# One vector per kind for the compressed branch's position terms, and tokens laid out by ScalarE straight from PSUM

## The chip, the core and the metric

The kernel runs on one core of one Trainium2 chip. Its time is the device time of one launch in microseconds (us). The profile shows one execution by engine: TensorE (PE, with its weight loads as PEld), VectorE (DVE), ScalarE (ACT), GpSimd (POOL) and SyncE (SP), which here only starts DMAs. A range like "745.00:775.00" is in us from the span's start.

## The reference, cut to what matters

The reference is one decoder layer for 1024 tokens of width 1024: a token mixer with three branches (stick-breaking attention, native sparse attention, a gated linear recurrence), then a feed-forward part that picks rows out of tables of 16384 experts (PEER), then a norm. The change touches one place: in sparse attention, keys and values for the compressed branch are made from overlapping blocks of 32 tokens, 16 apart. A learned position term is added to each block before it is multiplied with a weight:

```python
def compress(x, w):
    pieces = x.reshape(B, G, n_piece, CMP_STRIDE, dh)
    blocks = jnp.concatenate([pieces[:, :, j:j + n_cmp] for j in range(per)], axis=3) + cmp_pe
    return blocks.reshape(B, G, n_cmp, CMP_LEN * dh) @ w

kc = compress(k_cmp, w_cmp_k)
vc = compress(v_cmp, w_cmp_v)
```

Here B is 1, G is 2 (key groups), the head width dh is 64, CMP_STRIDE is 16 and CMP_LEN 32, so that there are 63 blocks, each a row of 2048 numbers times a weight of 2048 by 64. `cmp_pe` has 32 rows of 64 and is the same for every block and both groups.

## The kernel before, in words

**Two stages.** First a mixing stage: the tokens go through in four parts of 256 (`PARTS`), and for each part four rounds `r` of three kinds of items (`hg` the recurrence, `ns` the sparse attention, `sb` the stick-breaking attention) are worked off as a list of small items, while projections, merges, output products, top-k routing and, for parts 1 and 2 of 0 to 3 (`DENSE`), the spreading of the gates (`hot`, `gb`, `stage`) are emitted between them. Then a dense stage: for parts 1 and 2 all 128 blocks of experts are multiplied through (`gemm1`, whose result is the tile `g`, then `gemm2` into `acc`), while parts 0 and 3 have their expert rows gathered by GpSimd (lines 1149 and 1159) and used on VectorE (lines 1151 and 1161).

**What sets the order.** Python code emits the instructions in a planned order: pieces have a step by which they must be out (`before`), and a running account of modelled work for PE and DVE (`account`, `due`) decides how many optional pieces go into each step. The tile framework then schedules what was emitted by a timeline simulation at build time (`schedule_with_timeline_sim=True`, line 1567), so that the order on every engine depends on the modelled duration of everything emitted. At run time each engine works its queue in that fixed order. The VectorE work on gathered rows is placed among the mixing stage's VectorE work by `paced` (line 1119).

**Projections.** `proj` (line 268) loads a weight block in a high and a low half, and adds 24 matmuls of 128 by 256 into a PSUM tile of the pool `ps_mm`, which has two buffers. Such a buffer is free when its reader, mostly one ScalarE copy, is done; the next projection but one needs it.

**The piece that the change rewrites.** `nsa_kv_pieces` (line 470) makes a part's keys and values. `pieces(which)` (line 498, `which` 0 for keys and 1 for values) copies the projection into the tile `xc` (line 486, ScalarE) and then lays it out for the product in `xp` on VectorE (`add_pe`, line 510): 16 slots `j`, each of two tokens in the two halves of the partitions, for both groups and all blocks. Slots 0 to 7 hold a block's first 16 tokens and slots 8 to 15 its last 16, so each token is written twice, with another position term each time. That is eight VectorE instructions per kind and part, and four small ones more from part 1 on, for the 16 tokens kept in `xhist` from the part before (line 521). `compress` (line 523) then multiplies the 16 slots with the weight `cw` into `pk` and copies the result into `kcT` or `vcT` (line 527).

**ScalarE's tables.** The kernel keeps ScalarE on a table that holds exponential and logarithm (`log_exp`, line 95). `sigmoids` (line 889) is the exception: with high priority it applies sigmoids to the recurrence's `raw_hg` and `sg`, to the branch gates `gts` in a part's first round, and to the merge gates `mg`, and then asks for the exp-and-log table again (line 903). Wherever the final ScalarE order puts an exponential or logarithm between two of these sigmoids, a table load (ACT_TABLE_LOAD) stands before it, one for the exponential and another for the logarithm. The logits of stick-breaking attention need both in turn (`e_sb`, exponential at line 423 and logarithm at line 424, then a VectorE scan at line 429, and an exponential at line 433).

Of the kernel before, what the change touches and what calls it, by code (L numbers as in the profile page):

```python
# [10 lines left out]
F32 = mybir.dt.float32  # L11
# [5 lines left out]
AF = mybir.ActivationFunctionType  # L17
ALU = mybir.AluOpType
# [53 lines left out]
def trunk(ctx: ExitStack, tc: tile.TileContext, a: dict, out: bass.AP):  # L72
# [26 lines left out]
    def load(t, src):  # L99
        nc.sync.dma_start(t, src)  # L100
        return t
# [28 lines left out]
    packed = load(cst.tile([128, 273], F32, name="packed"), a["c_packed"])  # L130
    ident, rowv, iota16 = packed[:, 0:128], packed[:, 128:129], packed[:, 129:145]
    forced = packed[:, 145:273].rearrange("p (a b) -> p a b", a=8)
    small = load(cst.tile([128, 40], F32, name="small"), a["small"])
    peT, hnorm, hlb = small[:, 0:32], small[:, 32:36], small[:, 36:40]
    identb = cst.tile([128, 128], BF16, name="identb")
    V.tensor_copy(identb, ident)
    ones = cst.tile([128, 128], F32, name="ones")
# [60 lines left out]
    vcT = per.tile([64, 2, 64], F32, name="vcT")  # L198
    V.memset(kcT, 0.0)
    V.memset(vcT, 0.0)  # L200
    xhist = per.tile([128, 2, 16], F32, name="xhist")
    hgS = [per.tile([128, 128], F32, name=f"hgS{h}") for h in range(4)]
    for h in range(4):
        V.memset(hgS[h], 0.0)
# [265 lines left out]
    def nsa_kv_pieces(pt, st):  # L470
# [25 lines left out]
            st["cw", which] = load(W4(f"cw{which}_{nm}", (128, 16, 64)), a["wcmp"][which])  # L496

        def pieces(which):
            plain(B_NKV + which, f"xc{which}")
            xc = st[f"xc{which}"]  # L500
            xp = st["xp", which] = W2(f"xp{which}_{nm}", (128, 16, 2, np_), tag="xp", bufs=1)

            def add_pe(half, d0, nb, src):
                for g in range(2):
                    gs = slice(g * 64, g * 64 + 64)
                    for par in range(2):
                        o = xp[par * 64:par * 64 + 64, half * 8:half * 8 + 8, g, d0:d0 + nb]
                        i = src[gs].rearrange("p (c j u) -> p u j c", j=8, u=2)[:, par]
                        e = peT[gs, half * 16:half * 16 + 16].rearrange("p (j u) -> p u j", u=2)[:, par]
                        V.tensor_tensor(o, i, e.unsqueeze(2).to_broadcast([64, 8, nb]), op=ALU.add)  # L510


            if pt.first:
                add_pe(0, 0, np_ - 1, xc[:, 0:n - 16])
                add_pe(1, 0, np_ - 1, xc[:, 16:n])
            else:
                add_pe(0, 0, 1, xhist[:, which, :])
                add_pe(0, 1, np_ - 1, xc[:, 0:n - 16])
                add_pe(1, 0, np_, xc)
            if not pt.last:  # L520
                V.tensor_copy(xhist[:, which, :], xc[:, n - 16:n])

        def compress(which, dst):
            pk = ps_mm.tile([64, 2, np_], F32, tag="mm", name=f"pk{which}_{nm}")
            for j in range(16):
                P.matmul(pk[:, :, 0:ncb], st["cw", which][:, j, :], st["xp", which][:, j, :, 0:ncb], start=(j == 0), stop=(j == 15))
            V.tensor_copy(dst[0:64, :, c0:c1], pk[:, :, 0:ncb])

        def turn_values():
            pv = ps_mm.tile([64, 2, 64], F32, tag="mm", name=f"pvc_{nm}")  # L530
# [990 lines left out]
def _layout(inp):  # L1521

    d = {}
    w = np.asarray(inp["w_in"])[0]
    cols = []
    for o, n in ((0, 512), (512, 512), (1024, 512), (1536, 512), (2048, 768), (2816, 24), (2840, 512), (3352, 512), (3864, 512), (4376, 512), (4888, 3072)):
        x = w[:, o:o + n]
        if n == 24:
            x = np.concatenate([x, np.zeros((D, 104), w.dtype)], axis=1)
        cols.append(x)  # L1530
    cols += [np.asarray(inp["w_out"])[0], np.asarray(inp["peer_w_q"])[0]]
    w = np.concatenate(cols, axis=1)
    d["wblk"] = np.ascontiguousarray(w.reshape(8, 128, NBLK, 128).transpose(2, 1, 0, 3))
    br = np.stack([np.asarray(inp[n])[0] for n in ("w_branch_sb", "w_branch_nsa", "w_branch_hgrn")])
    d["wbr"] = np.ascontiguousarray(br.reshape(3, 4, 128, 8, 128).transpose(0, 3, 2, 1, 4).reshape(24, 128, 4, 128))
    cw = np.stack([np.asarray(inp[n])[0].reshape(16, 128, 64).transpose(1, 0, 2) for n in ("nsa_w_cmp_k", "nsa_w_cmp_v")])
    d["wcmp"] = np.ascontiguousarray(cw)
    pe = np.asarray(inp["nsa_cmp_pe"])[0].T
    small = [np.concatenate([pe, pe], axis=0), np.asarray(inp["hgrn_norm"])[0].reshape(4, 128).T, np.asarray(inp["hgrn_lower_bounds"])[0].reshape(4, 128).T]
    d["small"] = np.ascontiguousarray(np.concatenate(small, axis=1))  # L1540
    k = np.asarray(inp["peer_sub_keys"])[0]
    kk = np.zeros((128, 256), k.dtype)
    kk[0:64, 0:128] = k[0].T
    kk[64:128, 128:256] = k[1].T
    d["keysT"] = kk
    d["x"] = np.ascontiguousarray(np.asarray(inp["x"])[0])
    d["norm_mix"] = np.ascontiguousarray(np.asarray(inp["norm_mix"]))
    d["norm_ffn"] = np.ascontiguousarray(np.asarray(inp["norm_ffn"]))
    d["norm_final"] = np.ascontiguousarray(np.asarray(inp["norm_final"])[None])
    d["peer_u"] = np.ascontiguousarray(np.asarray(inp["peer_u"])[0])  # L1550
    d["peer_uT"] = np.ascontiguousarray(d["peer_u"].reshape(128, 128, 8, 128).transpose(0, 3, 2, 1))
    d["peer_v"] = np.ascontiguousarray(np.asarray(inp["peer_v"])[0])
    return d
# [17 lines left out]
```

## Time and profile before

| | |
|---|---|
| median of three runs | 3500.18 us (3494.5 to 3507.36) |
| the profiled execution's own time | 3511.97 us |
| its span, first to last instruction | 3510.2 us |
| PE busy | 3199.7 us, 91% |
| DVE busy | 3000.6 us, 85% |
| ACT busy | 1556.4 us, 44% |
| mean granted TensorE clock | 0.942 |
| first `gemm1` matmul (end of the mixing stage) | 2038.3 us |

Busy times of several engines overlap, so that they do not add up to the span. Matmuls are pipelined and the profile models their ends; an engine's busy share is therefore read stage by stage, beside what it waited for. The chain of waits follows the work back from the last instruction; where it runs through an instruction, that instruction's duration is at that moment what the end hangs on.

### The profile page before, as it was taken

To read this page: it belongs to the slowest core of one execution; us is meant where nothing else is said; L and a number is where in the kernel's file an instruction comes from. 1 tells how busy PE (TensorE), PEld (TensorE's weight loads), DVE (VectorE), ACT (ScalarE), POOL (GpSimd) and SP (SyncE) were. 2 spreads that over 40 slices of the span, in tenths; PEclk is the share of its full clock that TensorE was granted. 3 is DMA by queue.
4 is the path that set the end of the run, shared out by engine and by line. 5 is a ranking of instruction groups with operands and counts; after the bars stand their busy time and mean duration, and the time that the engine had idled before them with its cause. 6 is when DMAs were issued, how large, how long until landed. Compare 5 with 4: busy or idle time off the path is not lost.

```text
span 3510.2 us, 56907 instructions
## 1 busy us (share of the span) xinstructions
PE 3199.7 (91%) x20564; PEld 2175.3 (62%) x20564; DVE 3000.6 (85%) x6666; ACT 1556.4 (44%) x3181; POOL 1361.7 (39%) x1170
## 2 busy tenths in 40 slices
PE   7999889999997799999887889889999999999998
PEld 6887777778886688888565745434444444444443
DVE  6665679888789879889997869999988998998998
ACT  5776455554543554554455233333333333333333
POOL 0000002443332322333231334357765565676672
PEclk9999999999997799999688999989999999999999
DMA  8964856889976588897574998789999999999995
GB/s 305 334 248 147 308 185 226 320 314 310 358 284 231 199 289 291 327 332 259 191 250 154 344 372 312 241 271 387 392 384 329 385 367 362 362 368 375 367 358 219
DMA packets 359283, 1058.00 MB, mean 301 GB/s; under 512 B 35236, under 2 KB 107573, under 8 KB 354391
## 3 DMA queue, kind: packets, MB, share of 16 engines
q0 software_dynamic: 147456, 536.94, 42.5%
q1 hardware_dynamic: 206934, 483.87, 38.7%
q10 hardware_dynamic: 4608, 33.56, 2.5%
q8 instruction: 161, 2.64, 0.3%
q14 instruction: 124, 1.01, 0.1%
HBM read 944.13 MB, written 110.10 MB: 300 GB/s over the span
## 4 chain that ended last, share of the span: by engine, by line
PE 49%; DVE 23%; DMA 11%; issue 8%; ACT 6%; POOL 2%; SPq 0%; DVEq 0%; POOLq 0%; ACTq 0%
PE g L265 13%; PE acc L1441 10%; PE pj_mg L265 4%; DVE u L1151 3%; DVE gacc L1161 3%; PE g L1441 3%; DMA u<-in_peer_u_dram,gidx 3%; PE pj_r_hg L265 2%; DMA v<-in_peer_v_dram,gidx 1%; PE pb L265 1%; DMA gt<-d_G 1%; PE pj_wo L265 1%; POOL v L1159 1%; PE z_sb L417 1%; DMA vraw<-in_peer_v_dram 1%
## 5 line engine op out<-in xcount | busy, mean ns | idle before, releaser
L1159 POOL DMA_INDIRECT v<-in_peer_v_dram,gidx x421 | 556.0, 1321 | 674.0 <-DVE gacc L1161 348.4
L1149 POOL DMA_INDIRECT u<-in_peer_u_dram,gidx x417 | 529.7, 1270 | 596.6 <-DVE u L1151 367.4
L265 PE MATMUL g<-h,us 128*128 128x512 f16 x3072 | 688.2, 381 | 14.8 <-ACT ge L1400 12.1
L1441 PE MATMUL acc<-vs,ac 128*128 128x512 f16 x2304 | 542.2, 383 | 39.9 <-ACT vs L220 23.5
L1441 PEld LDWEIGHTS <-ac 128*128 128x128 f16 x3072 | 303.1, 99 | 426.1 <-issue 66.8
L1161 DVE SCALAR_TENSOR_TENSOR gacc<-v,act,gacc 128x1024 f32<-128x1024 f32 x421 | 538.9, 1280 | 29.4 <-DMA v<-in_peer_v_dram,gidx 25.8
L265 PEld LDWEIGHTS <-us 128*128 128x128 f16 x3072 | 301.6, 98 | 383.0 <-issue 21.1
L1151 DVE SCALAR_TENSOR_TENSOR u<-u,gh 128x1024 f32<-128x1024 f32 x417 | 501.9, 1219 | 33.2 <-DMA u<-in_peer_u_dram,gidx 32.7
L1400 ACT ACTIVATE ge<-g 128x512 f32<-128x512 f32 x128 | 76.1, 596 | 520.7 <-PE g L265 500.1
L265 PE MATMUL pj_mg<-hT,w_mg 128*128 128x256 f16 x2304 | 273.8, 275 | 4.0 <-ACT mg L885 4.0
L265 PEld LDWEIGHTS <-w_mg 128*128 128x128 f16 x2304 | 228.2, 100 | 33.6 <-issue 6.6
L1441 PE MATMUL g<-vs,ac 128*128 128x512 f16 x768 | 190.5, 388 | 11.6 <-ACT ge L1400 11.6
L1149 POOL DMA_INDIRECT rr_u<-in_peer_u_dram,gidx x95 | 134.2, 1413 | 96.7 <-DVE rr_u L1151 49.8
L221 DVE SCALAR_TENSOR_TENSOR vs<-vraw,vs 128x1024 f16<-128x1024 f32 x128 | 154.1, 1219 | 18.6 <-ACT vs L220 18.5
L221 DVE SCALAR_TENSOR_TENSOR us<-uraw,us 128x1024 f16<-128x1024 f32 x128 | 156.1, 1219 | 10.4 <-ACT us L220 10.3
L265 PE MATMUL pb<-o,w_b 128*128 128x256 f16 x1152 | 144.7, 281 | 21.1 <-DVE sg L923 15.1
L1159 POOL DMA_INDIRECT rr_v<-in_peer_v_dram,gidx x90 | 123.0, 1367 | 102.2 <-DVE gacc L1161 81.4
L220 ACT ACTIVATE vs<-vraw 128x1024 f16<-128x1024 f32 x128 | 131.0, 1046 | 55.0 <-DMA vraw<-in_peer_v_dram 55.0
L220 ACT ACTIVATE ac<-ge 128x512 f16<-128x512 f32 x128 | 79.9, 628 | 168.3 <-DVE ge L1434 139.0
L1434 DVE TENSOR_TENSOR ge<-ge,gt 128x256 f32<-128x256 f32 x256 | 98.4, 422 | 58.7 <-ACT ge L1400 44.9
L1223 PE MATMUL gb<-hot 128*128 128x128 f16 x512 | 125.7, 294 | 24.3 <-ACT stage L1226 13.1
L220 ACT ACTIVATE us<-uraw 128x1024 f16<-128x1024 f32 x128 | 134.2, 1048 | 21.4 <-PE g L265 12.8
(1146 smaller groups left out, 6353.8 us busy)
## 6 DMA issues: line engine op xcount, KB each, us to landing
uraw<-in_peer_uT_dram SPq DMA_DIRECT2D x128, 512.0 KB, 7.7
vraw<-in_peer_v_dram SPq DMA_DIRECT2D x128, 512.0 KB, 7.2
w_mg<-dw SPq DMA_DIRECT2D x72, 512.0 KB, 5.8
gt<-d_G SPq DMA_DIRECT2D x32, 1024.0 KB, 17.5
d_G<-stages ACTq DMA_DIRECT2D x20, 1024.0 KB, 5.9
w_r_hg<-dw SPq DMA_DIRECT2D x36, 512.0 KB, 5.4
w_b<-dw SPq DMA_DIRECT2D x72, 256.0 KB, 5.5
wr_mg<-in_wblk_dram SPq DMA_DIRECT2D x24, 512.0 KB, 5.3
```

The lines of the kernel that those rows point to most:

```text
L220: S.activation(hi, src, AF.Copy, scale=scale)
L221: V.scalar_tensor_tensor(lo, in0=src, scalar=scale, in1=hi, op0=ALU.mult, op1=ALU.subtract)
L265: P.matmul(ps, l[:, k, :], r[:, k, :], start=(i == 0), stop=(i == n - 1))
L417: P.matmul(x["z"], qz[:, hh, tl * 128:(tl + 1) * 128], st["k"][:, r0 + c0:r0 + c1], start=True, stop=(c0 > 0))
L1149: G.indirect_dma_start(out=ur, out_offset=None, in_=a["peer_u"], in_offset=bass.IndirectOffsetOnAxis(ap=idx[:, c:c + 1], axis=0))
L1151: V.scalar_tensor_tensor(ur, in0=ur, scalar=1.0, in1=h2, op0=ALU.mult, op1=ALU.mult, accum_out=hpre[:, c:c + 1])
L1159: G.indirect_dma_start(out=vr, out_offset=None, in_=a["peer_v"], in_offset=bass.IndirectOffsetOnAxis(ap=idx[:, c:c + 1], axis=0))
L1161: V.scalar_tensor_tensor(acc, in0=vr, scalar=act[:, c:c + 1], in1=acc, op0=ALU.mult, op1=ALU.add)
L1223: P.matmul(ps[:, n, :], hs[:, 0, :, n], hs[:, 2, :, n], start=True, stop=False)
L1400: S.activation(ge, ps, AF.Gelu, scale=1.0 / (SW * SH2))
L1434: V.tensor_tensor(gv, gv, gt[:, :, i % 8, :], op=ALU.mult)
L1441: P.matmul(ps, ac[:, x, t * 128:(t + 1) * 128], v[:, y, dh * 512:(dh + 1) * 512], start=start and n == 0, stop=stop and n == 2)
```

## The change

The position terms leave the layout. As the product is linear, the 32 position rows times the weight give one vector of 64 numbers per kind, the same for all blocks. It is computed once, in part 0 (`pc`, 16 matmuls with one column each, into `cpos`), and added when the product is taken out of PSUM: `tensor_scalar` in place of a copy, on VectorE as before. Without position terms a token looks the same in both halves of a block, so `xp` has 8 slots in place of 16 and one more column; slot `j` of the weight reads slot `j % 8`, shifted by one column for the second half. The layout is written by four ScalarE copies straight from the projection's PSUM tile, two groups by two token parities, with the scale in the copy, and `xc` is gone. The kept tokens are copied by ScalarE too: out of `xp` into `xhist`, and from there into column 0 of the next part's `xp`.

```diff
         def pieces(which):
-            plain(B_NKV + which, f"xc{which}")
-            xc = st[f"xc{which}"]
-            xp = st["xp", which] = W2(f"xp{which}_{nm}", (128, 16, 2, np_), tag="xp", bufs=1)
-
-            def add_pe(half, d0, nb, src):
-                for g in range(2):
-                    gs = slice(g * 64, g * 64 + 64)
-                    for par in range(2):
-                        o = xp[par * 64:par * 64 + 64, half * 8:half * 8 + 8, g, d0:d0 + nb]
-                        i = src[gs].rearrange("p (c j u) -> p u j c", j=8, u=2)[:, par]
-                        e = peT[gs, half * 16:half * 16 + 16].rearrange("p (j u) -> p u j", u=2)[:, par]
-                        V.tensor_tensor(o, i, e.unsqueeze(2).to_broadcast([64, 8, nb]), op=ALU.add)
...
+            ps = proj(B_NKV + which, hTs[pt.i], f"xc{which}_{nm}", pt)
+            d0 = 0 if pt.first else 1
+            xp = st["xp", which] = W2(f"xp{which}_{nm}", (128, 8, 2, np_ + 1), tag="xp", bufs=1)
+            if not pt.first:
+                S.activation(xp[:, :, :, 0], xhist[:, which], AF.Copy)
+            for g in range(2):
+                for par in range(2):
+                    o = xp[par * 64:par * 64 + 64, :, g, d0:d0 + np_]
+                    S.activation(o, ps[g * 64:g * 64 + 64].rearrange("p (c j u) -> p u j c", j=8, u=2)[:, par], AF.Copy, scale=PS)
             if not pt.last:
-                V.tensor_copy(xhist[:, which, :], xc[:, n - 16:n])
+                S.activation(xhist[:, which], xp[:, :, :, d0 + np_ - 1], AF.Copy)
 
         def compress(which, dst):
             pk = ps_mm.tile([64, 2, np_], F32, tag="mm", name=f"pk{which}_{nm}")
             for j in range(16):
-                P.matmul(pk[:, :, 0:ncb], st["cw", which][:, j, :], st["xp", which][:, j, :, 0:ncb], start=(j == 0), stop=(j == 15))
-            V.tensor_copy(dst[0:64, :, c0:c1], pk[:, :, 0:ncb])
+                P.matmul(pk[:, :, 0:ncb], st["cw", which][:, j, :], st["xp", which][:, j % 8, :, j // 8:j // 8 + ncb], start=(j == 0), stop=(j == 15))
+            if pt.first:
+                pc = ps_mm.tile([64, 1], F32, tag="mm", name=f"pc{which}")
+                for j in range(16):
+                    P.matmul(pc, st["cw", which][:, j, :], pos[:, j:j + 1], start=(j == 0), stop=(j == 15))
+                V.tensor_copy(cpos[:, which:which + 1], pc)
+            V.tensor_scalar(dst[0:64, :, c0:c1], pk[:, :, 0:ncb], cpos[:, which:which + 1], None, op0=ALU.add)
```

Because the order is made at build time, it moves elsewhere too. Three places are shown; lines after the change are those of the changed file, some six lower from line 510 on. In the names, trailing numbers count tiles; `e_sb_3_0_1_512` is a logit tile of part 3, `raw_hg_3` and `mg_3` are that part's recurrence inputs and merge gates.

**VectorE, keys of part 3.** Before:

```order
L221 SCALAR_TENSOR_TENSOR o_2_12357<-tro_ns2g_1_15346,o_2_12357 128x256
L510 TENSOR_TENSOR xp_ns_15480<-xc_ns_15478,small 64x8x15 x4
L510 TENSOR_TENSOR xp_ns_15480<-xc_ns_15478,small 64x8x16 x4
L1161 SCALAR_TENSOR_TENSOR gacc_33005<-v_98_33301,act_32617,gacc_33005 128x1024
L429 SCALAR_TENSOR_TENSOR e_sb_2_0_1_0_15330<-r_sb_2_0_1_0_15333,e_sb_2_0_1_0_15330 128x512
```

and after:

```order
L222 SCALAR_TENSOR_TENSOR o_2_12317<-tro_ns2g_0_15330,o_2_12317 128x256
L222 SCALAR_TENSOR_TENSOR o_2_12317<-tro_ns2g_1_15335,o_2_12317 128x256
L1213 TENSOR_TENSOR hot_15691<-iorep,spread_14070 128x1024
L430 SCALAR_TENSOR_TENSOR e_sb_2_0_1_0_15319<-r_sb_2_0_1_0_15322,e_sb_2_0_1_0_15319 128x512
L1214 TENSOR_TENSOR hot_15691<-hot_15691,spread_14070 128x1024
```

The eight layout instructions are gone, and the gates' spreading (`hot`) moves up into their place.

**ScalarE, sigmoids of part 3's second round.** Before:

```order
L902 ACT_TABLE_LOAD
L902 ACTIVATE raw_hg_3_14885<-raw_hg_3_14885 128x256
L902 ACTIVATE sg_3_17204<-raw_hg_3_14885 128x512
L902 ACTIVATE mg_3_16634<-mg_3_16634 128x1536
L97 ACT_TABLE_LOAD
L421 ACTIVATE e_sb_3_1_0_0_17245<-z_sb_3_1_0_0_17244 128x512
```

and after:

```order
L896 ACT_TABLE_LOAD
L896 ACTIVATE raw_hg_3_14874<-raw_hg_3_14874 128x256
L896 ACTIVATE sg_3_17188<-raw_hg_3_14874 128x512
L424 ACT_TABLE_LOAD
L424 ACTIVATE e_sb_3_0_1_512_17167<-e_sb_3_0_1_512_17167 128x384
L425 ACT_TABLE_LOAD
L425 ACTIVATE e_sb_3_0_1_512_17167<-e_sb_3_0_1_512_17167 128x384
L879 ACTIVATE mg_3_16613<-pj_mg_1_3_16767 128x256
L1220 ACTIVATE stage_16700<-gb_16811 128x128x4
L422 ACTIVATE e_sb_3_1_0_0_17229<-z_sb_3_1_0_0_17228 128x512
L423 ACTIVATE r_sb_3_1_0_0_17232<-z_sb_3_1_0_0_17228 128x512
L424 ACT_TABLE_LOAD
```

The merge gates' sigmoid no longer stands with the two others but 44 rows later, and exponentials and logarithms lie between, each behind a load. ScalarE's queue has 91 table loads before and 108 after; all 17 more are in the mixing stage.

**TensorE, keys of part 0, after:**

```order
L515 MATMUL pk_ns_644<-xp_ns_586,cw_ns_410 64x2x15 x8
L816 MATMUL pa_hg_0_504<-X_hg_0_485 128x64 x2
L515 MATMUL pk_ns_644<-xp_ns_586,cw_ns_410 64x2x15 x8
L816 MATMUL pa_hg_0_513<-X_hg_0_494 128x64 x2
L519 MATMUL pc_661<-small,cw_ns_410 64x1 x16
L816 MATMUL pa_hg_0_598<-X_hg_0_499 128x64 x2
```

The sixteen `pc` matmuls stand behind the sixteen `pk` of the same kind, in part 0 alone. On VectorE's queue 422 uses of gathered rows stand ahead of the dense stage's first product, before as after.

More of the change, by code (lines that the diff above doesn't have):

```diff
@@ L132, in trunk @@
     forced = packed[:, 145:273].rearrange("p (a b) -> p a b", a=8)
-    small = load(cst.tile([128, 40], F32, name="small"), a["small"])
-    peT, hnorm, hlb = small[:, 0:32], small[:, 32:36], small[:, 36:40]
+    small = load(cst.tile([128, 24], F32, name="small"), a["small"])
+    pos, hnorm, hlb = small[:, 0:16], small[:, 16:20], small[:, 20:24]
     identb = cst.tile([128, 128], BF16, name="identb")
@@ L200, in trunk @@
     V.memset(vcT, 0.0)
-    xhist = per.tile([128, 2, 16], F32, name="xhist")
+    xhist = per.tile([128, 2, 8, 2], F32, name="xhist")
+    cpos = per.tile([64, 2], F32, name="cpos")
     hgS = [per.tile([128, 128], F32, name=f"hgS{h}") for h in range(4)]
@@ L498, in pieces @@
         def pieces(which):
-            plain(B_NKV + which, f"xc{which}")
-            xc = st[f"xc{which}"]
-            xp = st["xp", which] = W2(f"xp{which}_{nm}", (128, 16, 2, np_), tag="xp", bufs=1)
-            def add_pe(half, d0, nb, src):
-                for g in range(2):
-                    gs = slice(g * 64, g * 64 + 64)
-                    for par in range(2):
-                        o = xp[par * 64:par * 64 + 64, half * 8:half * 8 + 8, g, d0:d0 + nb]
-                        i = src[gs].rearrange("p (c j u) -> p u j c", j=8, u=2)[:, par]
-                        e = peT[gs, half * 16:half * 16 + 16].rearrange("p (j u) -> p u j", u=2)[:, par]
[L510 to L519, printed above, removed]
+            ps = proj(B_NKV + which, hTs[pt.i], f"xc{which}_{nm}", pt)
[7 more added lines that the diff above has]
+                    S.activation(o, ps[g * 64:g * 64 + 64].rearrange("p (c j u) -> p u j c", j=8, u=2)[:, par], AF.Copy, scale=PS)
             if not pt.last:
-                V.tensor_copy(xhist[:, which, :], xc[:, n - 16:n])
+                S.activation(xhist[:, which], xp[:, :, :, d0 + np_ - 1], AF.Copy)
         def compress(which, dst):
@@ L1538, in _layout @@
     pe = np.asarray(inp["nsa_cmp_pe"])[0].T
-    small = [np.concatenate([pe, pe], axis=0), np.asarray(inp["hgrn_norm"])[0].reshape(4, 128).T, np.asarray(inp["hgrn_lower_bounds"])[0].reshape(4, 128).T]
+    small = [pe.reshape(64, 16, 2).transpose(2, 0, 1).reshape(128, 16), np.asarray(inp["hgrn_norm"])[0].reshape(4, 128).T, np.asarray(inp["hgrn_lower_bounds"])[0].reshape(4, 128).T]
     d["small"] = np.ascontiguousarray(np.concatenate(small, axis=1))
```

## The prediction

> **What bounds the kernel now.** I read the page's head first, then the two stages apart in the view of busy time by stretch, with the instructions of tile `g`, whose first start parts the stages.
>
> ```profile
> span 3510.2 us, 56907 instructions
> PE 3199.7 (91%) x20564; PEld 2175.3 (62%) x20564; DVE 3000.6 (85%) x6666; ACT 1556.4 (44%) x3181; POOL 1361.7 (39%) x1170
> ...
> L265 PE MATMUL g<-h,us x3072: 376/379/634, 2038.3 to 3475.3; 128*128 128x512 f16 x192
> ...
> 0.00:2038.00 2038.00, 1809.21 (x14098) 1535.86 (x14098) 1662.41 (x4524) 1065.54 (x2522) 496.86 (x559) 0.92 0.77 271
> 2038.00:3510.00 1472.00, 1390.47 (x6466) 639.40 (x6466) 1338.18 (x2142) 490.82 (x660) 864.85 (x611) 0.98 0.94 344
> ```
>
> The columns of a stretch are its length, the busy us of PE, PEld, DVE, ACT and POOL, the granted clock, the DMA share and GB/s. The dense stage, 1472 us with PE busy for 94% of it, holds nothing that the change edits, and as many gathered rows are left for it as before, so I give it no change. All that follows is about the mixing stage: PE 89% busy, DVE 82%, ACT 52%. No engine bounds it alone. PE leads, and its 229 us of idle time (2038 minus 1809) go to many short waits for the others. So a DVE microsecond is worth something only where DVE is last, and ACT is not free either.
>
> **What is removed from DVE.** The instructions of lines 510 and 486:
>
> ```profile
> L510 DVE TENSOR_TENSOR xp_ns<-xc_ns,small x64: 329/355/374, 52.2 to 1326.9; 64x120 f32<-64x120 f32 x40, 64x128 f32<-64x128 f32 x24
> L510 DVE TENSOR_TENSOR xp_ns<-xhist,small x24: 152/168/173, 70.4 to 1318.0; 64x8 f32<-64x8 f32 x24
> ...
>   PEld pk_ns L526: 1.3, 3
>   PE pk_ns L526: 0.5, 2
> ```
>
> ```profile
> L486 ACT ACTIVATE xc_ns<-pj_xc_ns x8: 362/383/420, 50.4 to 1323.2; 128x256 f32<-128x256 f32 x8
> L521 DVE COPY xhist<-xc_ns x6: 174/175/177, 55.2 to 787.6; 128x16 f32<-128x16 f32 x6
> ```
>
> 64 by 0.355 is 22.7 us, 24 by 0.168 is 4.0 and 6 by 0.175 is 1.1: 27.8 us. The eight products are still taken out of PSUM by one DVE instruction each, and two tiny copies of 0.17 us come in, so that 27.5 us net leave DVE. What waited directly for the layout is small: PE 0.5 us and its weight loads 1.3 us. But other work stood behind it in DVE's queue, and that is seen in the chain of waits, taken for 44 to 75, 325 to 365, 765 to 805 and 1300 to 1340 us, around the layouts of parts 0 to 3:
>
> ```profile
> by line: PE pj_xc_ns L265 25.6%; PE pa_hg L822 13.9%; PE pj_ksel_ns L265 8.8%; PE pj_kwin_ns L265 8.4%; DVE xp_ns L510 7.9%; PE pk_ns L526 6.8%; DVE X_hg L806 6.5%; issue 5.4%; ACT L97 4.1%; PE tr_vsel_ns L282 2.2%; PE pj_nq_ns0g L265 2.1%;
> by line: PE pj_nq_ns1g L265 13.1%; PE pj_xc_ns L265 11.0%; PE pj_ksel_ns L265 6.8%; PE pj_vwin_ns L265 6.6%; DVE xp_ns L510 6.0%; PE pb L265 6.0%; ACT X_hg L807 5.8%; issue 4.5%; PE pa_hg L822 4.4%; ACT mg L902 3.4%; ACT L902 3.2%; ACT L97
> by line: DVE u L1151 29.2%; DMA u<-in_peer_u_dram,gidx 20.5%; DVE xp_ns L510 15.6%; issue 7.3%; DVE X_hg L806 6.0%; DVE e_sb L429 5.7%; DVE X_hg L815 5.1%; DVE r_sb L432 3.2%; DVE o L221 2.5%; DVE b_hg L782 1.6%; DVE lf_hg L776 1.1%; ACT lf
> by line: PE pj_vwin_ns L265 13.2%; PE pk_ns L526 10.3%; PE z_sb L417 7.0%; PE ov_sb L447 6.9%; PE pj_ksel_ns L265 6.8%; PE pj_kwin_ns L265 6.6%; PE pj_xc_ns L265 6.5%; PE gb L1223 5.1%; PE gb L1224 4.7%; ACT mg L902 3.4%; ACT L433 3.2%; ACT
> ```
>
> `xp` has 7.9% of 31 us, 6.0% of 40, 15.6% of 40 and nothing that shows of the last 40: 2.4 + 2.4 + 6.2, or 11 us on the chain. What lay on it can't all be won, for in those stretches PE is close behind:
>
> ```profile
> 765.00:780.00 15.00, 10.50 (x76) 8.84 (x74) 13.75 (x29) 12.51 (x22) 6.10 (x5) 0.75 0.89 308
> 780.00:795.00 15.00, 15.00 (x130) 12.73 (x128) 14.71 (x41) 5.73 (x13) 4.89 (x5) 0.91 0.87 297
> 1325.00:1340.00 15.00, 15.00 (x140) 13.02 (x139) 14.87 (x23) 8.98 (x21) 5.53 (x4) 1.00 0.90 314
> ```
>
> PE is full in two of the three. I take half of the 11: **minus 5.5 us**, with ends at minus 27.5 (all of it counts, later rather than here, since the queue moves up) and 0.
>
> **What is added to ACT.** Of the kind that comes, a copy of 64 partitions by 128 elements out of PSUM with a stride, no row exists. The nearest are a contiguous read of 128 elements from PSUM, a read of 512 from PSUM with the order of the axes turned (line 1226), and a very short one:
>
> ```profile
> 1308.56 0.27 ACT L421 ACTIVATE e_sb<-z_sb 128x128 f32<-128x128 f32 x1
> ...
> 1319.21 0.60 ACT L1226 ACTIVATE stage<-gb 128x512 f32<-128x512 f32 x1 [0.67 <-PE gb L1224]
> ...
> 1297.19 0.21 ACT L539 ACTIVATE gts_ns<-tr_ng_ns 128x48 f32<-128x48 f32 x1
> ```
>
> The turned read costs 0.60 us for 512 elements, which the contiguous 0.27 for 128 doesn't undercut per element, so I charge the stride nothing. 32 by 0.27 is 8.6, the twelve copies of kept tokens 12 by 0.21 is 2.5, less 8 by 0.383 for `xc`: 8.0 us more on ACT, bounded by 32 by 0.60 (18.6 more). The projection's PSUM buffer is held for four copies in place of one, 0.7 us longer. What hides this is the next projection, which has the other buffer and takes 2.8 us; where the ACT queue is behind already, it adds to PE's wait. In all I put **plus 1 us** on the path, between 0 and 8.
>
> **What is added to PE.** `pc` is as many matmuls with the same weights as one product `pk`, with one column for 32:
>
> ```profile
> 1315.12 2.11 PE L526 MATMUL pk_ns<-xp_ns,cw_ns 128*64 128x32 f32 x32
> 53.71 1.01 PEld L526 LDWEIGHTS pk_ns<-xp_ns,cw_ns 128*64 128x64 f32 x16 [1.02 <-ACT X_hg L808]
> ```
>
> The 32 records are 16 matmuls of two passes. The weight loads alone, 16 in 1.01 us, give 2.0 us for 32, so fewer columns save next to nothing. Two kinds make 4.1 us, in part 0, where the chain above is mostly PE: **plus 4 us**, between 0 (in gaps) and 4.
>
> **What the new order adds.** ACT gets 17 more table loads, in groups where the sigmoids stand apart. One such load, what follows it, and two groups that exist before, of six loads (first and last shown) and of eight:
>
> ```profile
> 1698.16 1.28 ACT L902 ACT_TABLE_LOAD   x1
> 1699.45 0.42 ACT L902 ACTIVATE raw_hg<-raw_hg 128x256 f32<-128x256 f32 x1
> ...
> 473.16 1.28 ACT L902 ACT_TABLE_LOAD   x1
> ...
> 487.57 1.28 ACT L97 ACT_TABLE_LOAD   x1
> ...
> 747.76 1.28 ACT L902 ACT_TABLE_LOAD   x1
> ...
> 771.40 1.28 ACT L97 ACT_TABLE_LOAD   x1
> ```
>
> ```profile
> 470.00:495.00 25.00, 19.71 (x147) 16.25 (x147) 17.08 (x53) 21.45 (x30) 0.00 (x0) 0.93 0.52 175
> 745.00:775.00 30.00, 24.77 (x180) 19.02 (x179) 23.70 (x50) 27.45 (x47) 14.28 (x14) 0.96 0.84 288
> ```
>
> 17 by 1.28 is 21.8 us of ACT. How much of it PE feels: in these two stretches PE is idle 5.3 and 5.2 us. At the mixing stage's mean (229 in 2038, 11.2%) it would be 2.8 and 3.4, so the groups cost some 4.3 us. They hold 14 loads where two pairs, 4, would do: 0.43 us per load too many, times 17 is **plus 7.5 us**. The ends are 0 (all behind full PE) and 21.8 plus what a stall does to the clock. That price shows at 1309, where PE had waited 3.01 us on ACT: the next 24 matmuls took 5.28 us, against 2.78 for the same 24 in part 0, and the granted clock of 1300 to 1315 is 0.78.
>
> ```profile
> 1309.59 5.28 PE L265 MATMUL pj_vwin_ns<-hT,w_vwin_ns 128*128 128x256 f16 x24 [3.01 <-ACT vsel L491]
> 50.19 2.78 PE L265 MATMUL pj_vwin_ns<-hT,w_vwin_ns 128*128 128x256 f16 x24
> 1300.00:1315.00 15.00, 11.60 (x74) 8.60 (x72) 8.27 (x16) 11.03 (x24) 1.54 (x2) 0.78 0.54 186
> ```
>
> The Trainium skill, page "ScalarE: Activation LUTs", section "What ACT_TABLE_LOAD costs", puts a switch of tables at about 1283 ns for the load and 1380 more for a drain. This trace agrees on the load (1.28 us) and not on the drain, since the sigmoid starts 1.29 us after its load; by the page 17 switches would take 45 us of ACT, the term would be 15.5 in place of 7.5, and the sum plus 15. I keep the trace's.
>
> **Sum.** Minus 5.5, plus 1, plus 4, plus 7.5 is plus 7 us: a span of 3517 us for a profile like this one. The profiled execution took 3511.97 us, 12 more than the median of 3500.18, so the same step on the median gives **3507 us**, plus 0.2%. What a measurement of this kernel can tell from no change is about 0.5%, 17.5 us; the three runs lie 12.9 us apart.
>
> **The rivals.** *The freed DVE time comes through in full.* For it: DVE is at 14.7 to 14.9 of 15 us where the layouts of parts 2 and 3 stand, and GpSimd's gathers wait on DVE. Against: PE is full there too. Minus 27.5, plus 4 for `pc`, plus 1, with loads hidden to 2: minus 20, 3480 us. It decides from about four fifths of the 27.5 coming through. Chance 0.20.
>
> *ACT becomes the bound where the sigmoids stand apart.* The place is the logits of stick-breaking attention in parts 2 and 3, where exponential, logarithm, scan and exponential follow one another, each with a load ahead. For it: ACT is at 27.45 of 30 us in the old group of eight loads, and the new order has a group of twelve in 46 rows. Against: PE has projections to put in between. All 21.8 us, three stalls at 2.5 us of lost clock, plus 4, plus 1, minus 5.5: plus 29, 3529 us. From three fifths of it the kernel is measurably slower. Chance 0.25.
>
> *The change does not do what it says: DVE's time is freed where nobody waits.* Then minus 5.5 falls to 0 and the rest stays, plus 12.5: 3513 us. For it: part 3's chain has no `xp`, and the direct waits are under 2 us. Chance 0.15. My forecast keeps 0.40.
>
> **How the numbers follow.** Forecast and third rival both lie within 0.5%: 0.55. Faster has 0.20, slower 0.25. The range for 8 in 10 reaches the first rival and past the second, 3480 to 3535; the likeliest case alone has 3494 to 3517, from the half of the DVE term and of the loads' term that I chose.
>
> **What would show it.** DVE busy near 2973 us, ACT near 1586, PE plus 4. `g` first starts near 2045 and the dense stage keeps 1472 us: if it doesn't, my first step is wrong. `pc` takes 2.0 us per kind; a strided copy takes 0.27 us, and if it is near 0.6 the ACT term is wrong. PE's waits on ACT around the groups of loads in parts 2 and 3 decide between the forecast and the second rival; if the chain no longer runs through DVE near 770 to 790 us and the stage still ends no earlier, the DVE term was worth nothing.

## The result, and the profile after

The changed kernel takes **3543 us** (median, 3530 to 3555), the kernel before beside it 3502 us (3494 to 3507): a ratio of **1.0118, 95% interval 1.0078 to 1.0158**. It is slower, by about 41 us. The prediction, 3507 us with a range of 3480 to 3535, is wrong in size and misses at the slow end.

The page's head after:

```profile
span 3541.9 us, 57033 instructions
PE 3207.6 (91%) x20628; PEld 2181.2 (62%) x20628; DVE 2979.8 (84%) x6574; ACT 1585.9 (45%) x3234; POOL 1363.7 (39%) x1170
```

and the row of the dense stage's first products (count, ns of one as minimum, median and maximum, first and last start):

```profile
L266 PE MATMUL g<-h,us x3072: 376/379/634, 2066.8 to 3507.0; 128*128 128x512 f16 x192
```

The span is 31.7 us longer, 3541.9 against 3510.2. `g` starts at 2066.8 in place of 2038.3, so that 28.5 us of it arise in the mixing stage. To place them, the span is cut at five events that both kernels have: the merge gates' sigmoids of part 2's second round, of part 3's first and third, the last such sigmoids, and the first `g`. Busy time by stretch, columns as in the prediction (length, busy PE, PEld, DVE, ACT, POOL, clock, DMA share, GB/s), before:

```profile
0.00:904.30 904.30, 814.11 (x6738) 701.13 (x6739) 661.26 (x1884) 524.28 (x1246) 143.95 (x218) 0.96 0.77 272
904.30:1305.00 400.70, 356.19 (x2645) 302.62 (x2643) 355.21 (x1019) 191.91 (x492) 130.50 (x133) 0.88 0.76 271
1305.00:1568.20 263.20, 252.18 (x2064) 217.35 (x2063) 231.37 (x493) 140.49 (x338) 77.55 (x82) 0.97 0.87 308
1568.20:1821.50 253.30, 218.84 (x1478) 175.03 (x1476) 235.29 (x812) 120.35 (x273) 81.11 (x72) 0.85 0.68 228
1821.50:2038.30 216.80, 167.90 (x1182) 139.74 (x1180) 179.28 (x319) 88.78 (x179) 63.75 (x54) 0.83 0.75 271
2038.30:3510.20 1471.90, 1390.47 (x6466) 639.40 (x6466) 1338.18 (x2142) 490.54 (x659) 864.85 (x611) 0.98 0.94 344
```

and after:

```profile
0.00:897.80 897.80, 816.14 (x6811) 704.50 (x6812) 641.79 (x1808) 530.94 (x1282) 142.47 (x216) 0.96 0.78 272
897.80:1310.00 412.20, 360.46 (x2637) 306.42 (x2635) 356.51 (x1024) 201.05 (x494) 131.12 (x136) 0.86 0.77 266
1310.00:1575.60 265.60, 251.48 (x2079) 218.01 (x2077) 219.44 (x452) 149.35 (x342) 82.28 (x76) 0.97 0.84 294
1575.60:1851.10 275.50, 220.97 (x1459) 175.86 (x1458) 248.46 (x840) 125.31 (x283) 86.71 (x79) 0.84 0.68 229
1851.10:2066.80 215.70, 165.60 (x1188) 136.27 (x1185) 175.90 (x313) 88.88 (x180) 60.32 (x53) 0.86 0.74 263
2066.80:3541.90 1475.10, 1392.92 (x6466) 640.10 (x6466) 1337.66 (x2142) 490.38 (x659) 860.83 (x611) 0.98 0.94 343
```

Stretch by stretch the change is minus 6.5, plus 11.5, plus 2.4, **plus 22.2**, minus 1.1 and plus 3.2 us. The fourth holds part 2's scoring and routing. DVE is nearly full there (235 of 253 us before) and now has 13.2 us more to do, while in the third, where PE was the full engine (252 of 263), DVE has 11.9 us less. So DVE work has gone from a stretch in which DVE had 32 us to spare to one in which it had 18. A part of it is the use of gathered rows (line 1151 before, 1145 after). Its busy time on DVE in the same two stretches (length, busy DVE, clock, DMA share, GB/s), before:

```profile
1305.00:1568.20 263.20, 46.27 (x76) 0.97 0.87 308
1568.20:1821.50 253.30, 84.59 (x139) 0.85 0.68 228
```

and after:

```profile
1310.00:1575.60 265.60, 39.20 (x64) 0.97 0.84 294
1575.60:1851.10 275.50, 92.56 (x153) 0.84 0.68 229
```

It is 7.1 us less in the third stretch and 8.0 more in the fourth. In the fourth, DVE also waits longer. What DVE waited for there (total us, times, longest), before:

```profile
DVE e_sb L429 <- ACT e_sb L424: 4.3, 3, 1.8
...
DVE hot L1219 <- PE gb L1224: 0.8, 1, 0.8
```

and after:

```profile
DVE e_sb L430 <- ACT e_sb L425: 9.1, 3, 5.3
DVE hot L1213 <- PE gb L1218: 5.3, 3, 4.2
```

None of these instructions belongs to the code that the change rewrites. What does belong to it came as priced: a strided copy 0.276 us, a `pc` group 2.03 us (PE's timeline after, with start and duration):

```profile
53.92 2.03 PE L519 MATMUL pc<-small,cw_ns 128*64 128x1 f32 x32
```

The copies by line after, in ns as above:

```profile
L508 ACT ACTIVATE xp_ns<-pj_xc_ns x32: 271/276/282, 48.1 to 1328.9; 64x128 f32<-64x128 f32 x32
```

So the question for the experiments was what re-timed work that the change does not touch.

### The profile page after: what moved, and what is told of

The parts are those of the page before. It is cut to its first block, busy times and chain, and to the rows that moved or that the text cites. A ratio compares the mean times of both kernels' runs of the same rounds, so it can differ in the third digit from the quotient of the medians.

```text
span 3541.9 us, 57033 instructions
## 1 busy us (share of the span) xinstructions
PE 3207.6 (91%) x20628; PEld 2181.2 (62%) x20628; DVE 2979.8 (84%) x6574; ACT 1585.9 (45%) x3234; POOL 1363.7 (39%) x1170
## 5 line engine op out<-in xcount | busy, mean ns | idle before, releaser
L266 PEld LDWEIGHTS <-w_mg 128*128 128x128 f16 x2304 | 228.5, 100 | 31.7 <-issue 4.6
```

The lines of the kernel that those rows point to most:

```text
L266: P.matmul(ps, l[:, k, :], r[:, k, :], start=(i == 0), stop=(i == n - 1))
```

## The experiments

**How the instructions and the plan were taken apart.** With the layout gone from VectorE, `account` adds up less modelled work, so that more optional VectorE pieces fit into a step; and TensorE's allowance follows VectorE's work of the step. There are 748 pieces (projections, merges, scoring, routing, spreading, sigmoids), each with a step. The change moves 277 of them to other steps, and hardly any of these is edited: ahead of step 325, 103 pieces by plus 123 steps in sum (later); from step 325 on, shortly before part 3's items go out, 174 pieces by minus 275 (earlier). These counts go kind by kind; pl_p01's expectation counts in the order of emission, which gives 259 where the table has 59 and 174.

All kernels in one table. "Moved" is against the plan of the kernel before: pieces and sum of their steps ahead of step 325, and from it on. The ratio is to the kernel before, run beside each; there it had medians of 3502 to 3508 us, so that rows are best compared by their ratios. "Fourth stretch" is that of part 2's scoring, its length and DVE's busy time in it; "dense" is the time from the first `g` to the end. All three are from one profiled execution of each kernel.

| kernel | instructions | moved ahead of 325 | moved from 325 | table loads | us | ratio (95%) | fourth stretch, DVE | dense |
|---|---|---|---|---|---|---|---|---|
| before | before | 0 | 0 | 91 | 3502 | | 253.3, 235.3 | 1471.9 |
| the change | after | 103, +123 | 174, -275 | 108 | 3543 | 1.0118 (1.0078 to 1.0158) | 275.5, 248.5 | 1475.1 |
| e1 | after | 0 | 0 | 89 | 3513 | 1.0033 (1.0016 to 1.0050) | 252.6, 235.5 | 1476.1 |
| e1b, e1 again | after | 0 | 0 | 89 | 3514 | 1.0021 (1.0004 to 1.0039) | 253.2, 235.7 | 1456.2 |
| e3 | before | 103, +123 | 174, -275 | 102 | 3551 | 1.0141 (1.0117 to 1.0164) | 271.6, 244.7 | 1485.8 |
| n1 | before | 14, +14 | 0 | 91 | 3506 | 1.0006 (0.9991 to 1.0021) | 255.2, 234.9 | 1468.7 |
| e5 | after, sigmoids held | 103, +123 | 174, -275 | 93 | 3542 | 1.0129 (1.0085 to 1.0173) | 273.7, 247.4 | 1487.3 |
| f1 | after | 103, +123 | 106, -122 | 93 | 3523 | 1.0051 (1.0033 to 1.0069) | 254.6, 236.7 | 1466.9 |
| f2 | after | 103, +123 | 148, +62 | 109 | 3578 | 1.0217 (1.0181 to 1.0253) | 273.2, 249.0 | 1504.3 |
| f3 | before | 0 | 160, -229 | 87 | 3519 | 1.0034 (1.0014 to 1.0053) | 271.8, 248.4 | 1471.2 |
| pl_p01 | after | 59, +74 | 174, -275 | 102 | 3558 | 1.0138 (1.0096 to 1.0180) | 281.1, 248.6 | 1501.2 |
| g1 | after | 103, +123 | 174, -273 | 111 | 3550 | 1.0124 (1.0101 to 1.0146) | 269.5, 242.8 | 1487.1 |
| g2 | before | 0 | 1, -1 | 87 | 3506 | 1.0010 (0.9988 to 1.0032) | 257.9, 240.0 | 1465.2 |
| g3 | after, sigmoids held | 103, +123 | 174, -273 | 93 | 3530 | 1.0067 (1.0045 to 1.0089) | 262.3, 244.2 | 1488.5 |
| h1 | before | 13, +13 | 117, +175 | 90 | 3561 | 1.0162 (1.0133 to 1.0191) | 247.4, 230.1 | 1497.2 |
| h2 | before | 12, -16 | 130, -138 | 89 | 3522 | 1.0063 (1.0041 to 1.0085) | 263.5, 245.6 | 1469.5 |
| h3 | before | 89, +126 | 24, +16 | 95 | 3526 | 1.0067 (1.0044 to 1.0089) | 250.9, 237.3 | 1474.8 |
| h4 | after | 116, +136 | 95, +9 | 94 | 3527 | 1.0067 (1.0048 to 1.0086) | 249.6, 238.1 | 1492.8 |
| k1 | vector, layout on VectorE | 0 | 0 | 89 | 3509 | 0.9999 (0.9983 to 1.0014) | 255.8, 242.1 | 1476.6 |
| e7 | after, sigmoids held | 0 | 0 | 91 | 3530 | 1.0060 (1.0041 to 1.0078) | 261.5, 241.7 | 1472.2 |

**e1: the new instructions, the old plan.** The account is given the modelled time of the layout that is no longer there (and `cpos` and `pc` are taken out of it), so that every piece keeps its old step:

```diff
+            if pt.first:
+                load_["DVE"] += 8 * (0.06 + 120 / 960.0)
+            else:
+                load_["DVE"] += 4 * (0.06 + 8 / 960.0) + 4 * (0.06 + 120 / 960.0) + 4 * (0.06 + 128 / 960.0)
+            if not pt.last:
+                load_["DVE"] += 0.06 + 16 / 960.0
```

> The change with its new instructions, but the running account is given the VectorE time of the removed layout as if it were still there (and not the new vector's), so that every piece comes out in the same step as before the change. ScalarE's queue then has 89 table loads. If the plan is the cause (the account counts less VectorE work and so sends pieces out a step later), it runs at 3490 to 3502 us. If the table loads are the cause it is as fast, since they are gone with the plan. If the new instructions themselves cost it (strided ScalarE copies that hold PSUM, the vector's matmuls), it stays at 3535 to 3545.

**e3: the old instructions, the new plan.** The same terms with the other sign, in the kernel before.

> The kernel before, instruction for instruction, but the account is given what the changed kernel gives it, so that the pieces come out in the steps of the changed kernel. 102 table loads. The plan theory: 3530 to 3550 us, as slow as the change, with the old layout still on VectorE. The table-load theory: 11 of the 17 loads are there, so about two thirds of the loss, 3525 to 3532. The theory of the new instructions: 3497 to 3507, no change.

e1's third and fourth stretch:

```profile
1293.90:1554.60 260.70, 250.89 (x2067) 216.93 (x2065) 226.06 (x472) 141.61 (x345) 81.96 (x81) 0.98 0.87 310
1554.60:1807.20 252.60, 214.39 (x1473) 173.95 (x1471) 235.46 (x812) 120.41 (x273) 84.42 (x73) 0.86 0.68 229
```

and e3's:

```profile
1306.40:1578.90 272.50, 258.03 (x2091) 221.98 (x2092) 227.18 (x477) 143.27 (x333) 83.54 (x79) 0.95 0.83 294
1578.90:1850.50 271.60, 226.52 (x1460) 178.23 (x1458) 244.70 (x835) 124.85 (x284) 86.42 (x76) 0.82 0.66 225
```

e1 has the changed code and the old fourth stretch, 252.6 us; e3 has none of the changed code and the long one, 271.6 us. **The plan makes the loss**: it costs 30 us with the new instructions (3513 to 3543) and 50 with the old (3502 to 3551). With the old plan the new instructions cost about 10.

**e5: the change with the sigmoids held together.** This asks for the price that the prediction had put on the table loads. The sigmoids wait for the last copy into their merge gates, so that the group is not torn apart:

```diff
+            st["end"] = next(x for x in reversed(nc.cur_bb.bb.instructions) if x.engine == mybir.EngineType.Activation)
...
-        with tc.high_priority():
+        with tc.high_priority(), tc.issue_after(mg[0]["end"]) if mg else ExitStack():
```

> The change as it is, but ScalarE may start a group of sigmoids only after the last copy of the merge gates that belong to it, so that they stand together: 93 table loads in place of 108. If the loads are the cause: 3500 to 3512 us. If the plan is the cause by what it does to the order of VectorE and TensorE: 3530 to 3545, since 19 us of ScalarE time come back where it is not what is waited for.

The group in question, in the change, with the sigmoids and the first and last loads (start, duration):

```profile
1440.15 1.28 ACT L896 ACT_TABLE_LOAD   x1
1441.44 0.42 ACT L896 ACTIVATE raw_hg<-raw_hg 128x256 f32<-128x256 f32 x1
...
1442.40 1.28 ACT L424 ACT_TABLE_LOAD   x1
...
1469.09 1.28 ACT L896 ACT_TABLE_LOAD   x1
1470.39 1.49 ACT L896 ACTIVATE mg<-mg 128x1536 f32<-128x1536 f32 x1
```

The 35 us around it, after:

```profile
1440.00:1475.00 35.00, 27.41 (x204) 22.72 (x202) 26.85 (x41) 34.66 (x51) 12.21 (x11) 0.93 0.90 324
```

and before:

```profile
1440.00:1475.00 35.00, 30.92 (x223) 25.74 (x222) 24.14 (x40) 23.20 (x45) 10.19 (x9) 0.90 0.93 347
```

ACT is full there (34.7 of 35) and PE idles 7.6 us in place of 4.1. In e5 the time between the sigmoids of part 3's first and second round falls from 160.4 us to 149.9 (before: 151.9). So the loads do cost some 10 us at this place. But the kernel takes 3542 us with 15 loads fewer: what was won there is not seen at the end. e5's two stages in its profile:

```profile
0.00:2054.60 2054.60, 1808.44 (x14162) 1536.62 (x14162) 1639.90 (x4433) 1077.63 (x2560) 502.64 (x559) 0.92 0.76 269
2054.60:3541.90 1487.30, 1395.91 (x6466) 640.67 (x6466) 1338.19 (x2142) 489.59 (x659) 836.42 (x611) 0.97 0.93 340
```

The mixing stage ends 12.2 us earlier than the change's, and the dense stage, with the same work, takes 12.2 us longer. Whether the dense stage takes longer because of e5's order or by the scatter of single executions (20 us between e1 and e1b) is not shown. Nor is e5 a clean test of the loads: its edit has a price of its own, as e7 below shows.

**n1: a small nudge.** In the kernel before, the account is lowered once by 1.5 us in part 0; 14 pieces move by one step each.

> The kernel before, instruction for instruction, with a single nudge: in part 0 the account is given 1.5 us of VectorE work less, once. 91 table loads, as before. It asks how much time a nudge of the order moves by itself. If the loss of the change is a bias of the new plan, this stays within 10 us of before (3490 to 3512). If any new order of this kernel is drawn from a wide spread, it lies 15 us or more off, to either side.

Ratio 1.0006: so small a move costs nothing that can be measured.

**f1, f2, f3 and pl_p01: earlier or later, and where.** f1 and f2 raise the account of the changed kernel once, by 1.5 and 4.5 us, at step 325; f3 lowers that of the kernel before by 1.5 us; pl_p01 puts the layout's modelled time back in parts 0 and 1 alone.

```diff
         stepped[0] = t
+        if t == 325:
+            load_["DVE"] += 1.5
```

> The changed kernel with one number added: at step 325 of the plan, where part 3's items are about to be emitted, the account of modelled VectorE work is raised once by 1.5 us. All before that step is emitted as in the change. After it the optional pieces come back, on the mean over all pieces, to the steps that they have before the change (sum of the shifts against the kernel before: +1 step, where the change has -152). Theory A (the loss comes from VectorE pieces, above all the spreading of part 1's gates, that go out one to three steps earlier from part 3's items on): 3513 us, as with the old plan throughout, within 8 us either way. Theory B (any other order of this kernel costs tens of us by luck, and the old one happened to be a good draw): anything from 3500 to 3560, with no reason for 3513. Theory C (the loss comes from the plan's earlier parts): stays at 3543.

> The same with 4.5 us in place of 1.5: the optional pieces come later than before the change (sum of the shifts +185 steps). Theory A, if only too early is bad: 3505 to 3520 us. If it is the distance from the old steps that counts, in either direction: near 3540. Theory B: anything.

> The kernel before, with its own instructions, and the account lowered once by 1.5 us at step 325: the sum of the shifts is -229 steps, somewhat more than with the change, and 87 table loads on ScalarE's queue in place of 91. Theory A: slower, 3535 to 3555 us, as the old instructions were with the change's whole plan (3551). Theory B: anything. Theory C: 3500 to 3508, as the plan up to step 325 is untouched. If table loads are what costs: 3500 or less.

> The changed kernel with the removed VectorE layout's modelled time put back into the account in parts 0 and 1 alone. Its plan has 259 of 748 pieces at another step than the kernel before and 48 at another step than the change. Theory A: the part from step 325 on is the change's, so 3535 to 3550 us. Theory C: 3513. If table loads are what costs (102 here, against 108 in the change and 89 with the old plan): 3530.

f1 gives 20 of the 30 us back (its 3523 lies just above theory A's 3521), and its fourth stretch is about as long as before the change:

```profile
1573.50:1828.10 254.60, 216.63 (x1427) 173.91 (x1425) 236.64 (x817) 119.51 (x272) 83.61 (x72) 0.83 0.65 227
```

f2, with the pieces later than in the old plan, is the slowest of all. Theory A, that only too early is bad, falls with it. pl_p01 at 3558 keeps the late part of the change and the whole loss; f3, with the earlier part untouched, is 15 us slower. So theory C (the earlier parts alone) falls. f3's loss is less than theory A gave, though its fourth stretch (271.8 us) is nearly as long as the change's.

**g1, g2, g3: one piece.** In the runs so far a short fourth stretch went with the sigmoids of part 3's third round at step 383 or 384, a long one with 381 or 382. So that one piece was moved alone, from 382 to 384 in the changed kernel (g1), from 383 to 382 in the kernel before (g2), and to 384 together with the edit of e5 (g3).

```diff
-            sig = chain([...], -10, start[i, r, "hg"], p)
+            sig = chain([...], 380 if (i, r) == (3, 2) else -10, 384 if (i, r) == (3, 2) else start[i, r, "hg"], p)
```

> The changed kernel with one single piece of the plan moved: the sigmoids of part 3's third round go out at step 384; the change has them at 382, the kernel before at 383. All other 747 pieces keep the change's steps. In ScalarE's final order ten exponentials of part 3's sparse attention now stand between those sigmoids' merge gates and the ones before, as in the kernel before, where the change has six. So far the runs with the sigmoids at 383 or 384 had 131 to 135 us between the sigmoids of rounds 2 and 3 (counted from 0), those at 381 or 382 had 143 to 149. Theory D (this one position makes the late loss: more sparse attention falls into the stretch that is full of part 2's scoring on VectorE): the stretch goes back to 130 to 135 us and the kernel to 3520 to 3532 us. Theory E (the many pieces that come earlier make it, the sigmoids only mark it): 3537 to 3550.

> The kernel before, its own instructions, with the same single piece moved the other way: the sigmoids of part 3's third round at step 382 in place of 383, nothing else. Theory D: the stretch between the sigmoids of rounds 2 and 3 grows from 132 to 143 us or more and the kernel to 3512 to 3525. Theory E: 3498 to 3508.

> The changed kernel with both: the sigmoids held together behind their merge gates (93 table loads, which took the stretch from part 3's first to its second sigmoids from 160 back to 150 us) and the third sigmoids at step 384. Theory D with the loads as a second, separate term: both stretches are as before the change, 3510 to 3523 us, near the 3513 that the change takes with the old plan. Theory E: 3535 to 3545, as with the sigmoids together alone.

g1 takes 3550 us and g2 3506: the single piece is not the cause, and theory D falls. The fourth stretch of g1 stays long,

```profile
1569.90:1839.40 269.50, 219.69 (x1453) 175.82 (x1451) 242.78 (x823) 121.35 (x273) 87.19 (x78) 0.82 0.68 232
```

and that of g2 grows by 5 us. Yet g3, in which it moves along with the sigmoids held together, gains 12 us over e5 and at 3530 lies between the ranges of both theories. The effects of two moves do not add up.

**h1 to h4: four other plans.** Constants of the planner in place of a part of the change: VectorE's allowance per step 2.98 (h1) and 3.02 us (h2) in place of 3.0, and TensorE's 3.45 in place of 3.5 (h3), all in the kernel before; in the changed kernel VectorE's at 2.98 (h4).

```diff
-RPE, RDVE, REND, PD = 3.5, 3.0, 5.0, 1.2
+RPE, RDVE, REND, PD = 3.5, 2.98, 5.0, 1.2
```

> The kernel before, all instructions its own, with one constant of the planner changed: the VectorE allowance per step is 2.98 us in place of 3.0. From step 325 on 117 pieces move, by +175 steps in sum (later); before it 13 pieces by +13. Theory F (from step 325 on any displacement of the pieces, earlier or later, costs): 3512 to 3535 us. Theory A (only too early is bad): 3498 to 3508. Theory H (orders scatter about the old one in both directions, and the change drew a bad one): as likely below 3490 as above 3515.

> The kernel before with 3.02 us in place of 3.0: from step 325 on 130 pieces move by -138 steps in sum (earlier; the change moves 174 by -275), before it 12 by -16. Theory F: 3512 to 3535 us. Theory A: 3512 to 3540. Theory H: as likely below 3490 as above 3515.

> The kernel before with TensorE's allowance per step at 3.45 us in place of 3.5: ahead of step 325, 89 pieces move by +126 steps in sum, which is what the change does there (103 pieces, +123); from 325 on only 24 pieces by +16. Theories A and F (the loss is made from step 325 on): 3500 to 3510 us. If the earlier part has a share of the loss: 3515 or more. Theory H: as likely below 3490 as above 3515.

> The changed kernel with the VectorE allowance at 2.98 us, which takes back the earlier steps of the late part in sum (95 pieces moved by +9 against the kernel before; ahead of step 325, 116 by +136); 94 table loads. Theory A: 3508 to 3518 us. Theory F: 3515 to 3530, like the single 1.5 us at step 325 (3523). Theory H: anything from 3490 to 3560.

All four are slower than the kernel before, h1 by 1.6%, and at 3561 far above what theories A and F gave. Theory A falls again (h1 moves pieces later). H, by which half should have come out faster, has nothing for it, though four kernels are few. h3 moves hardly anything from step 325 on and loses 23 us; so the early part can cost too, and theory F, which put the loss on the late part alone, is too narrow. Nor is the fourth stretch always the place. h1's third, fourth and fifth stretch and its dense stage:

```profile
1300.80:1575.50 274.70, 259.95 (x2103) 224.86 (x2104) 232.85 (x490) 138.99 (x336) 78.63 (x81) 0.95 0.82 293
1575.50:1822.80 247.30, 209.32 (x1427) 170.27 (x1426) 230.03 (x801) 118.70 (x272) 78.36 (x69) 0.85 0.67 227
1822.80:2064.00 241.20, 181.49 (x1205) 146.55 (x1206) 190.12 (x337) 89.31 (x181) 67.17 (x61) 0.80 0.72 257
2064.00:3561.20 1497.20, 1397.49 (x6464) 640.20 (x6463) 1336.53 (x2139) 492.56 (x661) 845.15 (x610) 0.97 0.93 337
```

Its fourth is 6 us shorter than before the change; it loses 11.5 in the third, 24.4 in the fifth and 25.3 in the dense stage. The dense stage is long in other slow kernels too: it takes 1486 to 1504 us in eight of the twenty profiles, all of them kernels with a moved plan, and 1456 to 1477 in the other twelve. Its instructions were edited in none of them.

**e1b, k1, e7: what is left with the old plan.** e1b is e1 once more. k1 keeps the old plan, the vector and the 8 slots, but lets VectorE lay the tokens out of PSUM. e7 is e1 with the edit of e5.

```diff
-                    S.activation(o, ps[...], AF.Copy, scale=PS)
+                    V.tensor_scalar(o, ps[...], PS, None, op0=ALU.mult)
```

> The change with the old plan once more, with more rounds, beside the next two. Its first timing gave a ratio of 1.0033 to the kernel before (3513 against 3502 us). If the new instructions themselves cost something, again 3509 to 3517; if that was the scatter of the measurement, 3500 to 3508.

> One part of the change alone, with the old plan kept: the vector of position terms (pc, the added constant, 8 slots in place of 16), but the four layout copies per kind and part come out of PSUM on VectorE, with the scale, and so do the kept tokens; ScalarE loses the copies of xc and gets nothing. VectorE has about 12 us less than before the change in place of 27.5, ScalarE 12 us less than with the change. If the layout on ScalarE is what costs in the change with the old plan: 3498 to 3506. If pc does or nothing does: as e1b within 4 us.

> The change with the old plan and with the sigmoids held together behind their merge gates. With the change's own plan that shortened the stretch with the most table loads by 10 us; with the old plan there are 91 loads on ScalarE's queue against 89 without, so there is nothing to win: as e1b within 6 us. If holding them back makes the recurrence late: 3520 or more.

e1b shows a small loss again, 1.0021, with an interval that just excludes none; k1 is as fast as the kernel before, 0.9999, though its median of 3509 lies between the two cases that were expected. So the layout on ScalarE is the likelier half of what the instructions cost, but the two intervals overlap. e7 is slower than e1b by 16 us with the same plan and two table loads more: holding the sigmoids back, which shortened one stretch of the change, costs here. In e5 that price stood against whatever 15 loads fewer brought, so its unchanged time does not say that the loads are free. No kernel tried beats the one before.

## Why the prediction was wrong

**The failed step is "What the new order adds".** It priced the new order by its 17 table loads alone, plus 7.5 us (17 by 0.43 is 7.3). What the runs showed in its place is the plan's cost, 30 us with the new instructions. The number of loads does not set it: f3 and h1 have fewer than the kernel before and lose 15 and 57 us. That the loads carry a part of the change's own loss is not excluded: of the kernels with the new instructions, those with 102 loads or more take 3543 to 3578 us and those with 94 or fewer 3509 to 3542. But moved plans brought most of the loads with them, and no run took the loads away and nothing else. The rows on VectorE's order shown ahead of the prediction had `hot` in the place of the layout, and spreading is among the pieces that the account drew forward; the sum had no term for it. That optional pieces are drawn by modelled work stood in the description of the kernel, and that a change of modelled work re-times them all should have been a rival of its own.

**The DVE term (minus 5.5).** Its mechanism was there and its worth was not. DVE busy fell by 20.8 us, to 2979.8, where 2973 was forecast; the first stretch, with the layouts of parts 0 to 2, has 19.5 of it, and the 6.4 us of part 3's layout do not show in the sum of the later ones. The two stretches of 15 us near part 2's layout, which the prediction showed as nearly full of DVE, now read:

```profile
765.00:780.00 15.00, 9.71 (x68) 8.10 (x66) 9.45 (x20) 13.54 (x27) 6.58 (x5) 0.79 0.86 308
780.00:795.00 15.00, 15.00 (x132) 13.07 (x132) 11.68 (x27) 8.37 (x26) 3.12 (x4) 0.87 0.81 290
```

DVE is freed by 4.3 and 3.0 us, and PE gets 0.8 less and the same. The first stretch is 6.5 us shorter than in the execution of the kernel before, but g2, whose order is the old one up to there, has 894.9 us for it, less than the change's 897.8. So no gain is shown. With the plan held (e1, e1b) all instruction terms together make plus 8 to 11 us, where minus 5.5, plus 1 and plus 4 made minus 0.5. The first rival (3480 us) has nothing left for it.

**The ACT term (plus 1, ends 0 and 8)** had the right durations: 0.276 us a copy where 0.27 was taken, and ACT busy 1585.9 against a forecast near 1586. By k1 against e1b its place on the path is nearer to the upper end: 5 us of medians, not settled within the intervals. **The `pc` term** took 2.03 us per kind, as forecast.

**Table loads.** Each takes 1.28 us, and the sigmoid begins 1.29 us after its load starts. The Trainium skill, page "ScalarE: Activation LUTs", section "What ACT_TABLE_LOAD costs", adds a drain of some 1380 ns to the load; these rows again show none.

**The second rival (3529 us, chance 0.25)** was nearest in number, and its place exists: ACT at 34.66 of 35 us in part 3's second round, PE waiting 3.5 us more. e5 takes it away, and the mixing stage ends 12 us earlier, but the kernel is no faster. As e5's edit costs 16 us with the old plan, it does not settle how much this wait was worth. What is seen of it is 10 us at its place, a third of the plan's 30; e1 and e3 show that the loss comes with the plan, which this rival did not name. That it came near the number is in part luck.

**What held.** In the change's profile the dense stage is unchanged within what one program shows of itself (1475.1 against 1471.9 us); the difference arises in the mixing stage.

**What stays open.** Which of the moved pieces cost, and by what. In the change, 22 of 32 us lie where DVE work was pushed from a stretch bound by PE into one bound by DVE, and over the twenty profiles a fourth stretch over 260 us goes with 241 us of DVE work or more in it (k1 has 242 in one of 256); that is an observation, since no run moved that work alone. The gathered rows, whose uses are spread over the steps by modelled TensorE work, are the largest part of it that has a name (8.0 of 13.2 us); to pin them was not tried. Other plans lose elsewhere, some of them half of their loss in the dense stage, and why is not known. Theory B, that the old order was a good draw and most others cost tens of us, remains possible. What is shown is this: thirteen kernels have a plan that moves 100 pieces or more (the change itself among them). Twelve of them were slower than the same instructions with the old plan, by 10 to 65 us of medians (f1 and h4 within overlapping intervals), with pieces earlier or later, ahead of step 325 or behind it. The thirteenth, g3, takes the 3530 us that e7 takes with the old plan.

## What to carry to other kernels

Where a planner counts modelled work, taking instructions out also redraws the plan; ask first what the account will do with the freed time, and measure the two apart by feeding the account the old numbers. The price of a redrawn plan is to be had before any change, by moving a constant of the planner a little: here 0.7% in VectorE's allowance cost 19 us in one direction and 57 in the other, where the edit takes 27.5 us off VectorE in all. A local repair (a shorter stretch, fewer table loads, one piece put back) says nothing of the end until the whole kernel has been timed.

## What the runs showed that was not expected

One and the same program (e1 and e1b) had 1476 and 1456 us for its dense stage in two executions, while its mixing stage differed by 6: a stage's length in one profile is read to some 20 us there. A copy out of PSUM with a stride, 64 partitions by 128, took 0.276 us, as much as the contiguous one of 128 by 128 in the prediction (0.27): in these rows the stride cost nothing.
